# Two prices more in a kernel's scheduling model: VectorE's change of first partition and TensorE's change of weight width

## The chip, the cores and the metric

The kernel runs on one core of one Trainium2 chip. The metric is the device time of one execution in microseconds (us): 2971.12 as the median of three runs (2970.89 to 2973.47).

## What is computed

One layer of a decoder: a sequence of 2048 tokens of width 1024, a memory of 256 tokens. All is float32.

```
DEPTH = 1                                   # so layer 0 alone, the gated DeltaNet mixer
proj = x @ w_in                             # q, k, v, z (1024 each), a, b (8 each), mq (512)
qkv  = silu(causal_depthwise_conv(qkv, conv_w))
q, k = l2_normalize(q), l2_normalize(k)     # 8 heads of 128
o    = chunk_gated_delta_rule(q, k, v, g, beta)
       # in a chunk: A = I + strict_lower(beta k k^T * decay);  u = A^-1 v_beta,  w = A^-1 (k_beta e^g)
       # over chunks: state = state * dc + k_decay^T (u - w state)
o    = rms_norm(o, gate_norm_w) * silu(z)
m    = memory_attention(mq, mem_k, mem_v)   # 4 heads
x    = layer_norm(ALPHA * x + concat(o, m) @ w_out)
x    = layer_norm(ALPHA * x + square(relu(x @ w_ff1)) @ w_ff2)
```

## The kernel before

The tokens go through in four blocks of 512 (block 0 to 3). A block has a part of heads and a feed-forward part. In the heads part the projections aq, ak, av, az of eight heads (24 matmuls of 128x512 each, since every float32 product is made of three in float32r, from a high and a low part of each factor) alternate with small work of earlier heads. `dense` (line 671) makes a head's q, k, v, z; `gdn_a` (line 817) makes k k^T (pkq), the decays (dl, at) and calls `invert`; `gdn_b` (line 868) runs the recurrence over four chunks (pc, po, state). The memory attention (amq, sps, pmT, pmo) of four heads and the output projection (ao) fill in. The feed-forward part (af) uses a product scheme with seven instead of eight products.

`invert` (line 730) is the chain on which the prediction turns. VectorE copies blocks of L (tile dl) from four groups of 32 partitions into Lq, solves 16x16 blocks in fifteen steps of three operations (Bc, Bc, Xc), makes Z and its transpose ZT. Then three pairs of small matmul groups follow: pq = L-part times ZT, ScalarE copies pq to Q, pp = inverse-part times Q, and VectorE takes pp into ZT, Z, X, Y. The first pair has weights 112 columns wide, the second and third 64; all other matmul groups of the heads have 128. pp of the first pair needs Q and also XB, four copies of Z that ScalarE makes for four groups of 32 partitions. ScalarE makes much else in the same queue: the convolution's raw and scaled copies (raw, cq, ck, cv), squares with an accumulator (jq, jk), exponentials (dl, at, qd).

No engine's order is written by hand. Every operation is recorded (`Recorder.add`, line 147) with its engine, its tiles and a cost in ns; `Recorder.issue` (line 220) then plays the program through a model: it takes the engine that is free first, gives it the ready operation with the lowest number of recording, and notes start and end. An operation is ready when those that it depends on have ended plus a latency by pair of engines (`LAT`, `LAT_FROM`) and `MARGIN`. Tiles have so many buffers, and an operation waits for a free one. At the end all operations are sorted by modelled start (line 315) and emitted in this order (line 320), so that the model's times fix the order of each queue and nothing else. That is why every row of the profile has line 320. Semaphores make the real waits.

TensorE's cost is that of its columns plus, at a weight load, the time until the weights are in (lines 290 to 292). VectorE's is a constant and a price per element (line 211).

Of the kernel before, what the change touches and what calls it, by code (L numbers as in the profile page):

```python
# [14 lines left out]
P = 128  # L15
# [17 lines left out]
LAT = {("PE", "PE"): 0, ("DVE", "DVE"): 130, ("ACT", "ACT"): 155, ("POOL", "POOL"): 100}  # L33
LAT_FROM = {"PE": 200, "DVE": 130, "ACT": 135, "POOL": 75, "SP": 60}
MARGIN = 30


def _prod(v):
    r = 1
    for a in v:  # L40
        r *= a
    return r


class Buf:


    def __init__(self, pool, shape, dtype, tag, bufs, name):
        self.pool, self.shape, self.dtype, self.tag, self.bufs, self.name = pool, shape, dtype, tag, bufs, name
        self.ap = None  # L50
        self.psum = pool.name == "ps"
        self.users = 0
        self.end = 0
        self.held = False
        self.first = None
        self.log = []
# [7 lines left out]
class Ref:  # L64


    def __init__(self, buf, shape, steps=(), keys=None):
        self.buf, self.shape, self.steps, self.keys = buf, tuple(shape), steps, keys

    def _with(self, shape, *step):  # L70
        return Ref(self.buf, shape, self.steps + (step,), self.keys)

    def __getitem__(self, idx):
        ix = idx if isinstance(idx, tuple) else (idx,)
# [43 lines left out]
        return self._with(self.shape, "bitcast", (dt,), {})  # L118

    def part(self, *keys):  # L120
        return Ref(self.buf, self.shape, self.steps, frozenset(keys))

    def get(self):
        a = self.buf.get()
# [4 lines left out]

class Op:  # L130
    __slots__ = ("i", "eng", "fn", "args", "kw", "dur", "extra", "succ", "npred", "ready", "start", "end", "load", "last",
                 "bufs", "prio")


class Recorder:
# [11 lines left out]
    def add(self, eng, fn, name, args, kw):  # L147
        o = Op()
        o.i, o.eng, o.fn, o.args, o.kw = len(self.ops), eng, fn, args, kw
        o.succ, o.npred, o.ready, o.extra = [], 0, 0, 0  # L150
        o.prio = o.i + self.shift
        wr = [v for k, v in kw.items() if k in ("out", "accum_out")]
        rd = [v for k, v in kw.items() if k not in ("out", "accum_out")]
        rest = list(args)
        if "out" not in kw and rest:
            wr.append(rest.pop(0))
        rd += rest
        wr = [v for v in wr if isinstance(v, Ref)]
        rd = [v for v in rd if isinstance(v, Ref)]
        o.dur = self.cost(o, name, wr, rd, args, kw)  # L160
        preds = {}
        for refs, is_w in ((rd, False), (wr, True)):
            for r in refs:
                for q, qw, qk in r.buf.log:
                    if (is_w or qw) and (qk is None or r.keys is None or qk & r.keys):
                        preds[q.i] = q
        for refs, is_w in ((rd, False), (wr, True)):
            for r in refs:
                log = r.buf.log
                if is_w:  # L170
                    log[:] = [e for e in log if not (e[2] == r.keys or r.keys is None)]
                log.append((o, is_w, r.keys))
        for q in preds.values():
            q.succ.append(o)
        o.npred = len(preds)
        o.bufs = list({id(r.buf): r.buf for r in rd + wr}.values())
        for b in o.bufs:
            if b.first is None:
                b.first = o.i
            b.users += 1  # L180
        self.ops.append(o)

    @staticmethod
    def cost(o, name, wr, rd, args, kw):
        e = o.eng
        shapes = [r.shape for r in wr] + [r.shape for r in rd]
        n = max([_prod(s[1:]) for s in shapes] or [1])
        if e == "PE":
            rhs = kw.get("rhs", args[2])
            mo, n = _prod(args[1].shape[1:]), _prod(rhs.shape[1:])  # L190
            f32 = name == "transpose" or isinstance(rhs, Ref) and rhs.buf.dtype == F32
            o.load = 4 + 0.84 * mo
            o.last = 2.4 + 0.8334 * n if f32 else 13.4 + 0.4167 * n
            if name == "transpose":
                return o.last
            if f32:
                return o.last + max(o.last, o.load)
            return o.last
        psum = any(r.buf.psum for r in rd + wr)
        if e == "SP":  # L200
            o.extra = 1700 + _prod(wr[0].shape if wr else rd[0].shape) * 4 / 300.0
            return 450
        scal = [v for v in args[2:] if isinstance(v, Ref)] if name.startswith("tensor_scalar") else []
        scal += [v for k, v in kw.items() if k in ("scalar", "scalar1", "scale", "bias") and not isinstance(v, (int, float))]
        if e == "ACT":
            n = _prod((wr[0]).shape[1:])
            return 52 + 0.833 * n + (0 if psum else 42) + 93 * len(scal) + ((305 if scal else 198) if "accum_out" in kw else 0)
        if e == "DVE":
            fast = not psum and name in ("tensor_copy", "tensor_scalar_mul", "tensor_scalar_add", "tensor_scalar_max",
                                         "memset")  # L210
            return 68 + (0.52 if fast else 1.042) * n + 62 * len(scal) + (7 * n if name == "reciprocal" else 0)
        if name == "memset":
            return 40 + 0.83 * n
        if kw.get("op") == ALU.pow:
            return 300 + 165 * n
        if name == "tensor_copy":
            return 119 + 3.34 * n
        return 150 + 2.1 * n if name == "tensor_tensor" else 176 + 3.34 * n

    def issue(self):  # L220
# [3 lines left out]
        free = {e: 0.0 for e in engs}  # L224
        soon = {e: [] for e in engs}
        avail = {e: [] for e in engs}
        dma = [0.0]
        slots = {k: [0.0] * v[0].bufs for k, v in self.tags.items()}
        order = {k: sorted((b for b in v if b.users), key=lambda b: b.first) for k, v in self.tags.items()}
        pos = {}  # L230
# [18 lines left out]
        def place(o):  # L249
            for b in o.bufs:  # L250
                if not b.held:
                    if len(slots[b.key]) <= ahead(b):
                        wait[b.key].append(o)
                        return
                    b.held = True
                    b.since = heapq.heappop(slots[b.key])
                    again(b.key)
                o.ready = max(o.ready, b.since)
            heapq.heappush(soon[o.eng], (o.ready, o.i, o))

        def again(k):
            if wait[k]:
                w, wait[k] = sorted(set(wait[k]), key=lambda q: q.i), []
                for q in w:
                    pending.append(q)
# [4 lines left out]
        while True:  # L270
            while pending:
                place(pending.pop(0))
            best = None
            for e in engs:
                if avail[e]:
                    t = free[e]
                elif soon[e]:
                    t = max(free[e], soon[e][0][0])
                else:
                    continue  # L280
                if best is None or t < best[0]:
                    best = (t, e)
            if best is None:
                break
            t, e = best
            while soon[e] and soon[e][0][0] <= t:
                r, i, o = heapq.heappop(soon[e])
                heapq.heappush(avail[e], (o.prio, i, o))
            o = heapq.heappop(avail[e])[2]
            if e == "PE":  # L290
                t = max(t, fed + o.load)
                fed = t + o.dur - o.last
            o.start, o.end = t, t + o.dur
            free[e] = o.end
            if o.extra:
                dma[0] = max(o.end + 1700, dma[0]) + o.extra - 1700
                o.end = dma[0]
            out.append(o)
            for s in o.succ:
                lat = LAT.get((e, s.eng), LAT_FROM[e])  # L300
                if lat:
                    lat += MARGIN + (s.load if s.eng == "PE" else 0)
                s.ready = max(s.ready, o.end + lat)
                s.npred -= 1
                if s.npred == 0:
                    pending.append(s)
            for b in o.bufs:
                b.users -= 1
                b.end = max(b.end, o.end)
                if b.users == 0:  # L310
                    heapq.heappush(slots[b.key], b.end + LAT_FROM[e] + MARGIN)
                    again(b.key)
# [24 lines left out]
def hybrid_layer(  # L337
# [632 lines left out]
    def keep_sums(u, j):  # L970
# [9 lines left out]
        for i, o, x, y in ((1, 0, 1, 0), (3, 1, 3, 1), (2, 3, 3, 0), (4, 2, 2, 3)):  # L980
# [7 lines left out]
             ("S4", "B22", "A", True, (0, 1)))  # L988

    def ff_seven(b, ff1_tiles, relu2, add, norm2):  # L990
        Q = 2 * P
        for g in range(NS):
# [276 lines left out]
```

## Time and profile before

| | |
|---|---|
| median of 3 runs | 2971.12 us |
| the profiled execution | 2967.86 us |
| its span, first to last instruction | 2966.1 us |
| TensorE matmul busy | 2922.6 us, 99% |
| TensorE weight loads busy | 2410.1 us, 81% |
| VectorE busy | 2178.7 us, 73% |
| ScalarE busy | 1518.2 us, 51% |
| GpSimd busy | 342.1 us, 12% |
| chain that ended last: TensorE / VectorE / ScalarE | 81% / 8% / 7% |

A busy TensorE is not one at its peak: ends of matmuls are modelled, and they overlap. Where it matters, starts are compared. A wait is put down to the engine whose semaphore came last.

### The profile page before, as it was taken

To read this page: it belongs to the slowest core of one execution; us is meant where nothing else is said; L and a number is where in the kernel's file an instruction comes from. 1 tells how busy PE (TensorE), PEld (TensorE's weight loads), DVE (VectorE), ACT (ScalarE), POOL (GpSimd) and SP (SyncE) were. 2 spreads that over 40 slices of the span, in tenths; PEclk is the share of its full clock that TensorE was granted. 3 is DMA by queue.
4 is the path that set the end of the run, shared out by engine and by line. 5 is a ranking of instruction groups with operands and counts; after the bars stand their busy time and mean duration, and the time that the engine had idled before them with its cause. 6 is when DMAs were issued, how large, how long until landed. Compare 5 with 4: busy or idle time off the path is not lost.

```text
span 2966.1 us, 43768 instructions
## 1 busy us (share of the span) xinstructions
PE 2922.6 (99%) x15172; PEld 2410.1 (81%) x15172; DVE 2178.7 (73%) x5568; ACT 1518.2 (51%) x3582; POOL 342.1 (12%) x872
## 2 busy tenths in 40 slices
PE   8999999999999999999999999999999999999998
PEld 6888778888788878888888878888878887888886
DVE  7899887666888876665588777755668877675667
ACT  6666535444456652554545555344454556444443
POOL 2222100000122201000022220000001221000000
PEclk9999999999999999999999999999999999999999
DMA  8655577555733322544473333244456333324444
GB/s 283 238 192 178 192 237 234 194 190 181 278 136 121 121 100 79 158 146 137 154 258 135 122 111 100 89 144 148 149 168 244 125 122 111 100 86 149 145 146 135
DMA packets 127709, 469.84 MB, mean 158 GB/s; under 512 B 14464, under 2 KB 16896, under 8 KB 109056
## 3 DMA queue, kind: packets, MB, share of 16 engines
q1 hardware_dynamic: 126912, 467.00, 47.1%
q8 instruction: 119, 1.95, 0.3%
q14 instruction: 102, 0.84, 0.1%
q10 hardware_dynamic: 576, 0.06, 0.0%
HBM read 402.97 MB, written 64.03 MB: 157 GB/s over the span
## 4 chain that ended last, share of the span: by engine, by line
PE 81%; DVE 8%; ACT 7%; DMA 2%; issue 2%; POOL 1%; ACTq 0%; POOLq 0%; DVEq 0%
PE af L320 40%; PE ao L320 6%; PE az L320 5%; PE av L320 5%; PE ak L320 4%; PE aq L320 4%; PE amq L320 3%; PE pc L320 3%; DVE y L320 2%; PE pp L320 2%; PE pq L320 2%; PE po L320 2%; PE pkq L320 1%; DVE whl L320 1%; PE sps L320 1%
## 5 line engine op out<-in xcount | busy, mean ns | idle before, releaser
L320 DVE TENSOR_TENSOR whl<-wraw,whl 128x1024 fp32r<-128x1024 f32 (+1 forms) x446 | 541.4, 1216 | 462.6 <-ACT whl L320 460.9
L320 ACT CAST whl<-wraw 128x1024 fp32r<-128x1024 f32 (+1 forms) x446 | 466.6, 1046 | 371.7 <-PE af L320 202.6
L320 PE MATMUL af<-Thi,whl 128*128 128x512 f32 (+1 forms) x2304 | 649.8, 366 | 4.6 <-DVE whl L320 2.7
L320 PEld LDWEIGHTS af<-Thi,whl 128*128 128x128 f32 x2304 | 416.8, 189 | 76.0 <-DVE whl L320 3.7
L320 PE MATMUL af<-whl,xh 128*128 128x512 f32 x1536 | 474.8, 390 | 1.3 <-DVE whl L320 0.7
L320 PE MATMUL af<-Tlo,whl 128*128 128x512 f32 (+1 forms) x1152 | 421.1, 366 | 0.0
L320 PE MATMUL af<-whl,xl 128*128 128x512 f32 x896 | 346.0, 389 | 0.0
L320 PEld LDWEIGHTS af<-whl,xh 128*128 128x128 f32 x1536 | 287.8, 188 | 67.4 <-ACT whl L320 3.7
L320 PEld LDWEIGHTS af<-Tlo,whl 128*128 128x128 f32 x1152 | 217.3, 189 | 35.1
L320 PE MATMUL ao<-whl,ch 128*128 128x512 f32 x768 | 245.2, 397 | 0.3 <-DVE y L320 0.3
L320 ACT ACTIVATE rl<-af 128x512 f32<-128x512 f32 x128 | 76.5, 598 | 277.1 <-PE af L320 275.2
L320 PEld LDWEIGHTS af<-whl,xl 128*128 128x128 f32 x896 | 168.2, 188 | 34.4
L320 PE MATMUL aq<-Thi,whl 128*128 128x512 f32 x512 | 181.7, 412 | 7.2 <-ACT Thi L320 7.2
L320 PE MATMUL az<-Thi,whl 128*128 128x512 f32 x512 | 177.3, 406 | 1.1 <-DVE whl L320 1.1
L320 PE MATMUL av<-Thi,whl 128*128 128x512 f32 x512 | 176.6, 406 | 0.0
L320 PE MATMUL ak<-Thi,whl 128*128 128x512 f32 x512 | 173.5, 403 | 0.0
L320 PEld LDWEIGHTS ao<-whl,ch 128*128 128x128 f32 x768 | 143.1, 188 | 27.9 <-issue 1.4
L320 PE MATMUL ao<-whl,cl 128*128 128x512 f32 x384 | 156.2, 407 | 0.0
L320 DVE SCALAR_TENSOR_TENSOR y<-y,af 128x512 f32<-128x512 f32 x224 | 146.2, 677 | 8.7 <-PE af L320 8.7
L320 POOL MEMSET Y<- 128x512 f32 x32 | 16.8, 525 | 1037.9 <-PE af L320 921.0
L320 PEld LDWEIGHTS aq<-Thi,whl 128*128 128x128 f32 x512 | 94.7, 190 | 22.3 <-ACT Thi L320 7.2
L320 PEld LDWEIGHTS az<-Thi,whl 128*128 128x128 f32 x512 | 93.9, 189 | 17.3 <-DVE whl L320 1.5
(251 smaller groups left out, 5747.2 us busy)
## 6 DMA issues: line engine op xcount, KB each, us to landing
wraw<-in_w_ff_dram SPq DMA_DIRECT2D x224, 512.0 KB, 4.0
whl<-wsc SPq DMA_DIRECT2D x108, 1024.0 KB, 4.8
wraw<-tsc SPq DMA_DIRECT2D x128, 512.0 KB, 3.4
wsc<-whl SPq DMA_DIRECT2D x36, 1024.0 KB, 4.8
wraw<-in_w_out_dram SPq DMA_DIRECT2D x48, 512.0 KB, 4.2
wraw<-in_w_in_dram SPq DMA_DIRECT2D x35, 512.0 KB, 5.8
wq<-in_w_ff_dram SPq DMA_DIRECT2D x64, 256.0 KB, 4.4
tsc<-wq SPq DMA_DIRECT2D x64, 256.0 KB, 3.8
```

What stands on the lines that cost most here:

```text
L320: o.fn(*[res(a) for a in o.args], **{k: res(v) for k, v in o.kw.items()})
```

## The change

Two constants are added, DRAIN = 90 and SWITCH = 95 ns. A reference to a tile (`Ref`) now keeps the first partition of its slice (p0). An operation notes for its reads and writes, PSUM and SBUF apart, in which group of 32 partitions they begin (`quads`), and a matmul how many columns its weights have (`cols`). In `issue`, TensorE's start is put off by 95 ns when the width differs from that of the matmul before, and a VectorE operation whose group differs from the last one on the same side starts 90 ns after the engine is free. ScalarE, GpSimd and the queues are modelled as before.

```diff
+DRAIN, SWITCH = 90, 95
...
     def _with(self, shape, *step):
-        return Ref(self.buf, shape, self.steps + (step,), self.keys)
+        p0 = self.p0
+        if step[0] == "__getitem__":
+            ix = step[1][0]
+            ix = ix[0] if isinstance(ix, tuple) else ix
+            p0 += ix.indices(self.shape[0])[0] if isinstance(ix, slice) else 0
+        return Ref(self.buf, shape, self.steps + (step,), self.keys, p0)
...
+        o.quads = {("r" if v in rd else "w", v.buf.psum): v.p0 // 32 for v in wr + rd[::-1]}
...
-            o.load = 4 + 0.84 * mo
+            o.load, o.cols = 4 + 0.84 * mo, mo
...
+        quads, cols = {}, P
...
             if e == "PE":
+                if o.cols != cols:
+                    t += SWITCH
+                    cols = o.cols
                 t = max(t, fed + o.load)
                 fed = t + o.dur - o.last
+            if e == "DVE":
+                if any(quads.get(k, q) != q for k, q in o.quads.items()):
+                    t = max(t, free[e] + DRAIN)
+                quads.update(o.quads)
```

The instructions are the same in kind and number; their order differs in the heads of every block. Three places of block 3 follow, each as it was and as it is.

TensorE, first head of block 3, from its av projection to the first pair of the inversion (pq, then pp, 112 wide), before:

```order
L320 MATMUL av<-Tlo,whl 128x512
L320 MATMUL pq<-ZT_22859,LB 112x16 x4
L320 MATMUL av<-Thi,whl 128x512
L320 MATMUL az<-Thi,whl 128x512
L320 MATMUL az<-Tlo,whl 128x512
L320 MATMUL pp<-Q,XB 112x16 x4
L320 MATMUL az<-Thi,whl 128x512 x2
```

and now:

```order
L336 MATMUL av<-Tlo,whl 128x512
L336 MATMUL av<-Thi,whl 128x512
L336 MATMUL pq<-ZT_22859,LB 112x16 x4
L336 MATMUL az<-Thi,whl 128x512
L336 MATMUL az<-Tlo,whl 128x512
L336 MATMUL az<-Thi,whl 128x512 x2
L336 MATMUL az<-Tlo,whl 128x512
L336 MATMUL pp<-Q,XB 112x16 x4
```

The last av stands ahead of pq now, and five az instead of one av and two az stand between pq and pp.

ScalarE, at the same place (XB and Q are what pp waits for; raw and cv belong to the av projection), before:

```order
L320 COPY XB<-Z_22842 32x4x32 x2
L320 ACTIVATE th<-ck 128x512
L320 COPY XB<-Z_22842 32x4x32 x2
L320 COPY Q<-pq 112x4x16
L320 CAST kq<-ck 128x512
L320 COPY raw<-av 128x512
L320 ACTIVATE cv<-av,cw 128x512
```

and now:

```order
L336 COPY XB<-Z_22842 32x4x32 x2
L336 ACTIVATE th<-ck 128x512
L336 COPY XB<-Z_22842 32x4x32
L336 COPY raw<-av 128x512
L336 COPY XB<-Z_22842 32x4x32
L336 ACTIVATE cv<-av,cw 128x512
L336 COPY Q<-pq 112x4x16
L336 CAST kq<-ck 128x512
```

raw and cv have moved ahead of Q.

ScalarE, fourth head of block 3, the same copies (joss and jq are squares with an accumulator, on is the scaled output of an earlier head), before:

```order
L320 ACTIVATE joss,oss<-po 128x128
L320 ACTIVATE dl<-dl,gc 128x128
L320 COPY XB<-Z_23983 32x4x32
L320 ACTIVATE dl<-dl,gc 128x128
L320 COPY XB<-Z_23983 32x4x32
L320 ACTIVATE jq,ss<-ptq 128x128
L320 COPY XB<-Z_23983 32x4x32
L320 ACTIVATE jq,ss<-ptq 128x128
L320 COPY XB<-Z_23983 32x4x32
L320 ACTIVATE on<-po,ro 128x128
L320 COPY Q<-pq 112x4x16
```

and now:

```order
L336 ACTIVATE joss,oss<-po 128x128
L336 COPY XB<-Z_23977 32x4x32
L336 ACTIVATE dl<-dl,gc 128x128
L336 COPY XB<-Z_23977 32x4x32
L336 ACTIVATE dl<-dl,gc 128x128
L336 COPY XB<-Z_23977 32x4x32
L336 COPY Q<-pq 112x4x16
L336 ACTIVATE at<-at,ngc 128x128
L336 COPY XB<-Z_23977 32x4x32
L336 ACTIVATE jq,ss<-ptq 128x128
L336 ACTIVATE on<-po,ro 128x128
```

The two jq and on stand behind Q now, and one dl stands among the copies instead of ahead of them.

## Rows read from the trace of the kernel before

**Rows 1.** The page, busy us, share of the span and instructions by engine:

```profile
PE 2922.6 (99%) x15172; PEld 2410.1 (81%) x15172; DVE 2178.7 (73%) x5568; ACT 1518.2 (51%) x3582; POOL 342.1 (12%) x872
```

**Rows 2.** Windows (us), busy of PE, PEld, DVE, ACT, POOL, clock, DMA, GB/s:

```profile
480.00:720.00 240.00, 240.00 (x1060) 198.82 (x1059) 161.38 (x226) 116.34 (x157) 0.00 (x0) 1.00 0.61 198
...
2280.00:2520.00 240.00, 236.91 (x1428) 194.30 (x1427) 191.04 (x764) 140.40 (x490) 53.74 (x141) 1.00 0.34 122
```

**Rows 3.** Waits of TensorE, 2250 to 2590 us: us, times, longest:

```profile
PE pp L320 <- ACT Q L320: 1.4, 3, 0.6
PE pq L320 <- DVE Xc L320: 0.4, 1, 0.4
```

**Rows 4.** Waits of TensorE, 790 to 1130 us:

```profile
PE pq L320 <- DVE Bc L320: 0.4, 1, 0.4
```

**Rows 5.** Waits of TensorE, 60 to 400 us:

```profile
PE pp L320 <- ACT Q L320: 1.3, 3, 0.5
```

**Rows 6.** Waits of the weight loads, whole kernel:

```profile
PEld pp L320 <- ACT Q L320: 9.5, 15, 1.0
...
PEld pq L320 <- DVE Z L320: 3.2, 9, 0.7
```

**Rows 7.** Timeline of TensorE, a group 64 wide: start, us, operation, idle before:

```profile
2303.38 0.39 PE L320 MATMUL az<-Thi,whl 128*128 128x512 f32 x1
2303.70 0.65 PE L320 MATMUL pp<-Q,X 128*64 128x32 f32 x8
2304.28 0.50 PE L320 MATMUL az<-Thi,whl 128*128 128x512 f32 x1
2304.62 0.39 PE L320 MATMUL az<-Tlo,whl 128*128 128x512 f32 x1
```

**Rows 8.** Timeline of TensorE, first head of block 3, groups 112 wide:

```profile
2298.14 0.93 PE L320 MATMUL pq<-ZT,LB 128*112 128x16 f32 x8 [0.39 <-DVE Xc L320]
...
2299.47 0.40 PE L320 MATMUL az<-Tlo,whl 128*128 128x512 f32 x1
2299.70 0.87 PE L320 MATMUL pp<-Q,XB 128*112 128x16 f32 x8
2300.42 0.71 PE L320 MATMUL az<-Thi,whl 128*128 128x512 f32 x2
2300.97 0.40 PE L320 MATMUL az<-Tlo,whl 128*128 128x512 f32 x1
```

**Rows 9.** Timeline of VectorE, copies from groups of 32 partitions:

```profile
2291.15 0.27 DVE L320 COPY Lq<-dl 32x128 f32<-32x128 f32 x1
2291.29 0.20 DVE L320 TENSOR_TENSOR Xc<-Xc,Bc 128x52 f32<-128x52 f32 x1
2291.52 0.27 DVE L320 COPY Lq<-dl 32x128 f32<-32x128 f32 x1
```

**Rows 10.** Timeline of ScalarE, first head of block 3:

```profile
2299.11 0.21 ACT L320 COPY Q<-pq 112x64 f32<-112x64 f32 x1
...
2299.87 0.58 ACT L320 COPY raw<-av 128x512 f32<-128x512 f32 x1
2300.34 0.69 ACT L320 ACTIVATE cv<-av,cw 128x512 f32<-128x512 f32 x1
```

**Rows 11.** Timeline of ScalarE, fourth head of block 3:

```profile
2387.96 0.40 ACT L320 ACTIVATE dl<-dl,gc 128x128 f32<-128x128 f32 x1
2388.37 0.30 ACT L320 COPY XB<-Z 32x128 f32<-32x128 f32 x1
...
2389.21 0.29 ACT L320 COPY XB<-Z 32x128 f32<-32x128 f32 x1
...
2390.36 0.37 ACT L320 ACTIVATE on<-po,ro 128x128 f32<-128x128 f32 x1
```

**Rows 12.** Timeline of TensorE, fourth head of block 3:

```profile
2389.76 0.61 PE L320 MATMUL aq<-Thi,whl 128*128 128x512 f32 x2
2390.89 0.86 PE L320 MATMUL pp<-Q,XB 128*112 128x16 f32 x7 [0.52 <-ACT Q L320]
```

More of the change, by code (lines that the diff above doesn't have):

```diff
@@ L64, with __init__ @@
 class Ref:
-    def __init__(self, buf, shape, steps=(), keys=None):
-        self.buf, self.shape, self.steps, self.keys = buf, tuple(shape), steps, keys
+    def __init__(self, buf, shape, steps=(), keys=None, p0=0):
+        self.buf, self.shape, self.steps, self.keys, self.p0 = buf, tuple(shape), steps, keys, p0
     def _with(self, shape, *step):
-        return Ref(self.buf, shape, self.steps + (step,), self.keys)
+        p0 = self.p0
[4 more added lines that the diff above has]
+        return Ref(self.buf, shape, self.steps + (step,), self.keys, p0)
     def __getitem__(self, idx):
@@ L120, in part @@
     def part(self, *keys):
-        return Ref(self.buf, self.shape, self.steps, frozenset(keys))
+        return Ref(self.buf, self.shape, self.steps, frozenset(keys), self.p0)
     def get(self):
@@ L131 @@
     __slots__ = ("i", "eng", "fn", "args", "kw", "dur", "extra", "succ", "npred", "ready", "start", "end", "load", "last",
-                 "bufs", "prio")
+                 "bufs", "prio", "quads", "cols")
 class Recorder:
```

## The prediction

> **What bounds the kernel now.** I read the busy shares first, then windows by stage, then who waits for whom, then timelines of the places where a wait ends. TensorE is busy for 99% of the span, VectorE 73%, ScalarE 51% [rows 1]. The windows show two kinds of stage: in a feed-forward window TensorE is busy for 240.00 of 240 us and starts 1060 matmuls, one per 0.226 us; in a window of the heads it is busy 236.91 of 240 us [rows 2]. The granted clock is 1.00 in both, the 2.4 GHz level. So a better order can win something only in the heads, where TensorE waits for small chains: the inversion of a 128x128 block alternates matmul groups (pq, pp) with copies by ScalarE (Q, XB, Y) and with VectorE. From the order of the changed kernel this can be sharpened: on TensorE the feed-forward parts of blocks 1 to 3 stand row for row as before. What moves is the work of the heads.
>
> Who waits there: in the heads of block 3 the pp matmuls wait for ScalarE's Q three times, 1.4 us in all and 0.6 at most, and pq once for VectorE, 0.4 us [rows 3]; block 2 has the order of block 3. Block 1 does not wait for Q at all and 0.4 us at pq [rows 4], block 0 waits 1.3 us for Q [rows 5]. These are idle times left after modelled matmul ends. Weight loads, whose idle time starts earlier, show 9.5 us for Q and 3.2 us for VectorE's Z over the whole kernel [rows 6]. The truth lies between: at 2298.14 the page writes 0.39 us of idle, and at 2390.89 0.52 us [rows 8, 12]; the latter pp starts 1.13 us after a row of two matmuls began at 2389.76, and two matmuls take 0.45, so 0.68 was lost. A wait thus costs about 1.3 times its idle row.
>
> **The change part by part.** No instruction is added or removed; two prices are added to the model whose start times fix each engine's order.
>
> VectorE, 90 ns when the first partition changes. Normally a VectorE instruction starts before the one ahead of it ends: Xc at 2291.29 starts 0.13 us before the Lq copy of 2291.15 ends. The next Lq copy, from other partitions, starts at 2291.52, 0.03 us after Xc ended at 2291.49 [rows 9]. The change of partition costs 0.16 us against that neighbour, so the 90 ns are real and rather low. Some ten such changes per head (four Lq copies, two each of X32 and Y, one or two of X64 and of what follows) make about 1 us that the model left out and now has. [...]
>
> TensorE, 95 ns when the width of the weights changes. Around a group 64 wide, from the matmul at 2303.38 to the second one behind it at 2304.62, pass 1.24 us; two wide matmuls are 0.45 of it, the group from its start to its successor's 0.58, so 0.21 us goes for switching in and out against a charge of 0.19 [rows 7]. Around a group 112 wide, from 2299.47 to 2300.97, three wide matmuls are 0.68, the group 0.72, so 0.10 us is left against the same 0.19 [rows 8]. The 64-wide price is right, the 112-wide one about 0.09 us too high, twice a head. The Trainium skill, "TensorEngine Tiling (Array Packing)", section "Key Properties", says that a change of the tiling mode drains TensorE. A width of 112 needs no mode other than 128, so by this rule the charge there is unearned; the row, at half of the 64-wide cost, leans that way. The time that this would give is the slower rival below.
>
> What follows for the order, site by site in block 3 (block 2 has the same order):
>
> First head, TensorE and ScalarE. One av matmul moves ahead of pq, and five az matmuls instead of one av and two az stand between pq and pp. The wait of pq (0.39 us idle) loses up to 0.23. But ScalarE now puts raw and cv ahead of Q. Their runs are 0.58 and 0.69 us [rows 10]; some 1.1 to 1.3 us later than 2299.11 Q starts at 2300.2 to 2300.4 and ends 0.21 later. From Q's end at 2299.32 to pp at 2299.70 nothing was idle, so pp was not waiting; with two more matmuls in front it is due at 2300.15. It will wait 0.3 to 0.5 us. Net: a loss of 0.1 to 0.3, I take 0.2.
>
> Fourth head, ScalarE. Ahead of Q two jq with their accumulator reads, one on and one XB go; one dl comes in between. From 2388.37 to 2389.21 an XB with a jq takes 0.84, an XB alone runs 0.30, so a jq with its read takes 0.54; dl takes 0.41 to its successor, on runs 0.37 [rows 11]. The last XB, which pp needs as well, follows Q now. Up to its end 2 x 0.54 + 0.37 goes, one dl of 0.41 and one at of its kind come: 0.6 us earlier. TensorE has the same 1.1 us of work between pq and pp. The 0.52 us of idle [rows 12] goes; what is late next is pq two groups on, which has the X copies of VectorE ahead of it. Gain 0.5.
>
> Sixth head: ScalarE's order is as before, but one amq matmul more stands ahead of pq and one more between pq and pp, 0.45 us of cover against a wait of 0.4 to 0.6. Gain 0.4. Second head: order and wait stay, 0. In sum -0.7 us idle for a block, -1.4 for blocks 2 and 3.
>
> Block 1 had an order of its own without these waits and now gets that of blocks 2 and 3: it takes on the second head's 0.5, +0.5. Block 0: three waits, 1.3 us; the new order has more TensorE work ahead of pp at two of them. I take half, -0.7. Together -1.6 us of idle, times 1.3 is -2.1. The other small waits of the heads (pkq, pc, ptq) are shuffled with no reason that I can see for either sign; a chain that starts with more cover in most heads speaks for a little gain, and I take -3 in all. Bounds: if every wait of pq and pp went as the weight loads show them, 9.5 + 3.2, -12.7; if all that the 112-wide groups are overcharged became waiting, 0.09 x 2 x 32 = +5.8, and three first heads' 0.5 on top, +7.
>
> The profiled execution took 2967.86 us, 1.76 more than its span; the median of the runs is 2971.12, 3.3 above it. -3 gives 2964.9 in the first and 2968 in the second, and 2968 is the forecast.
>
> **The rivals.** Larger gain: with VectorE's prices right, most waits of the heads go, those of pkq and pc too, since they hang on the same late chain. For it: about 1 us per head was missing in the model and pq waits for VectorE only. Against it: the larger part of the wait is ScalarE's (9.5 against 3.2), and ScalarE is not charged for partition changes, though its jq with its accumulator read shows 0.54 us. Time: -7 to -13, centre 2961.
>
> Nothing: the model's two omissions, 1 us of VectorE and four 64-wide groups at 0.21, that is 0.84 us of TensorE per head, had nearly cancelled, and the new order is just another one. 2970 to 2973.
>
> Slower: ahead of the inversion's first two groups the model now thinks TensorE 0.09 us later per 112-wide group than it is, so that TensorE reaches pp early while Q is late; with raw and cv ahead of Q, as in the first head, in other heads too. It decides where pp has no slack of 0.2 us. Price +5.8 with the gains gone, up to +10: centre 2978.
>
> **How the numbers follow.** Forecast case 0.36, larger gain 0.31, nothing 0.13, slower 0.20. A measurement can tell 0.2%, 5.9 us, from no change. The larger gain lies wholly beyond that, the forecast case with 0.06 of its 0.36: faster 0.37. Slower 0.20 lies beyond on the other side. Within: 0.30 + 0.13 = 0.43. The range of the forecast alone is 2964 to 2971; with the two outer cases, until no more than 2 in 10 is out, 2956 to 2979.
>
> **What would show it.** Right: the fourth and sixth head of blocks 2 and 3 lose their idle before pp, the first head's pq waits less and its pp newly waits 0.3 to 0.5 us, block 1 looks like 2 and 3, and the feed-forward windows keep 0.226 us per matmul. Wrong: waits for Q as long as before or longer in the heads (then ScalarE's missing price or the 112-wide charge rules), or waits of pkq and pc that move by more than 2 us in total (then my shuffle term was not small).

## The result, and the profile after

The changed kernel took 2982.42 us (median of 5 runs, 2974.86 to 2987.02) against 2970.89 us for the kernel before in the same comparison: a ratio of 1.0037, 95% interval 1.0023 to 1.0052. It is slower by 0.4%, where 2968 us and a small gain were forecast. A second comparison gave 2979.08 us (8 runs; ratio 1.0026, 1.0014 to 1.0038); the median of all 13 is 2981.0. The profiled execution was the slowest of the first five, 2987.02 us, span 2985.3.

The page's busy line, which answers to [rows 1]:

```profile
PE 2933.9 (98%) x15172; PEld 2417.6 (81%) x15172; DVE 2179.3 (73%) x5568; ACT 1521.9 (51%) x3582; POOL 348.3 (12%) x872
```

The windows of [rows 2], with the same columns:

```profile
480.00:720.00 240.00, 240.00 (x1060) 198.70 (x1059) 162.38 (x228) 117.86 (x161) 0.00 (x0) 1.00 0.62 198
2280.00:2520.00 240.00, 236.51 (x1377) 194.67 (x1375) 195.53 (x773) 140.02 (x474) 52.07 (x139) 0.99 0.36 127
```

The feed-forward window is as it was, 1060 matmuls in 240 us. The window of the heads holds 1377 matmuls instead of 1428, and its granted clock is 0.99; the heads of block 3 begin 14 us later now, so the two windows do not hold the same stretch of them.

Waits of TensorE in the heads of block 3 (2265 to 2607 us), which answer to [rows 3]:

```profile
PE pp L336 <- ACT Q L336: 1.4, 3, 0.7
PE pkq L336 <- ACT jq L336: 0.9, 1, 0.9
PE ptq L336 <- ACT kd L336: 0.5, 1, 0.5
PE pp L336 <- ACT XB L336: 0.3, 1, 0.3
PE pq L336 <- DVE Bc L336: 0.2, 1, 0.2
```

Q is waited for exactly as long as before, 1.4 us in three places, which is the first of the signs by which the prediction said it would be wrong. pkq waited 0.4 us before and waits 0.9; ptq and a pp that waits for XB have come in addition. Blocks 1 and 2 have nearly the same rows.

The place of [rows 8, 10], the first head of block 3, ScalarE and then TensorE:

```profile
2314.34 0.29 ACT L336 COPY XB<-Z 32x128 f32<-32x128 f32 x1
2314.64 0.59 ACT L336 COPY raw<-av 128x512 f32<-128x512 f32 x1
2315.24 0.29 ACT L336 COPY XB<-Z 32x128 f32<-32x128 f32 x1
2315.55 0.69 ACT L336 ACTIVATE cv<-av,cw 128x512 f32<-128x512 f32 x1
2316.14 0.20 ACT L336 COPY Q<-pq 112x64 f32<-112x64 f32 x1
```

```profile
2314.02 0.93 PE L336 MATMUL pq<-ZT,LB 128*112 128x16 f32 x8 [0.22 <-DVE Bc L336]
...
2315.81 0.39 PE L336 MATMUL az<-Tlo,whl 128*128 128x512 f32 x1
2316.39 0.37 PE L336 MATMUL pp<-Q,XB 128*112 128x16 f32 x2 [0.19 <-ACT Q L336]
```

This is what was foretold: raw and cv stand ahead of Q, pq waits 0.22 instead of 0.39 us, and pp newly waits.

The second head of block 3, ScalarE and TensorE, where nothing was foretold:

```profile
2334.59 0.28 ACT L336 ACTIVATE jq<-ptq 128x128 f32<-128x128 f32 x1
2334.88 0.20 ACT L336 ACTIVATION_READ_ACCUMULATOR jq<-ptq 128x1 f32 x1
```

```profile
2333.75 0.47 PE L336 MATMUL aq<-Thi,whl 128*128 128x512 f32 x1
2335.14 0.38 PE L336 MATMUL pkq<-kq 128*128 128x256 f32 x1 [0.91 <-ACT jq L336]
```

pkq takes the PSUM bank that ptq had, so that the last jq must have read it. One aq matmul stands between pq and pkq; from its start to pkq pass 1.39 us, 1.16 more than it takes. That stands in blocks 1 to 3, 3.5 us together.

Where the time went can be read from starts: from the last af of one feed-forward part to the first af of the next is one part of heads. Block 1, before and in the second profile of the changed kernel (changed_again below):

```profile
777.44 0.39 PE L320 MATMUL af<-whl,xl 128*128 128x512 f32 x1
...
1164.18 0.28 PE L320 MATMUL af<-Thi,whl 128*128 128x256 f32 x1
```

```profile
781.97 0.39 PE L336 MATMUL af<-whl,xl 128*128 128x512 f32 x1
...
1174.31 0.28 PE L336 MATMUL af<-Thi,whl 128*128 128x256 f32 x1
```

That is 386.7 us before and 392.3 now. The heads of blocks 0 to 3 took 438.0, 386.7, 390.8 and 389.3 us before; 442.4, 392.3, 392.2 and 390.7 in this profile of the changed kernel, and 441.8, 395.5, 393.7 and 394.1 in the first. The feed-forward parts differ by 1.0 us at most. With half of every stretch at the lower clock taken out, block 1 lost 3.7 to 3.9 us and blocks 2 and 3 lost 1.2 to 1.4 each. Block 0 lost some 4, a part of it clock; its largest new waits (ao waited 0.3 us before and pto not at all) are these:

```profile
PE ao L336 <- DVE y L336: 2.3, 3, 1.5
PE pto L336 <- ACT on L336: 2.1, 2, 1.9
```

I use two measures below. The lost time of a group is its start minus the start of the matmul ahead, less what that one takes undisturbed (0.226 us for 128x512). The clock share of a run is its time times one minus its granted clock, which is what the lower level (1.2 GHz, shown as 0.5) takes from a TensorE that is always busy; a mean over the runs is given, since the clock is listed to 0.001. In every profile 5 to 9 us of it lie at the kernel's start and end, so only differences of it are read.

### The profile page after: what moved, and what is told of

It reads as the page before. It is cut to its first block, busy times and chain, and to the rows that moved or that the text cites. A ratio compares the mean times of both kernels' runs of the same rounds, so it can differ in the third digit from the quotient of the medians.

```text
span 2985.3 us, 43767 instructions
## 1 busy us (share of the span) xinstructions
PE 2933.9 (98%) x15172; PEld 2417.6 (81%) x15172; DVE 2179.3 (73%) x5568; ACT 1521.9 (51%) x3582; POOL 348.3 (12%) x872
## 4 chain that ended last, share of the span: by engine, by line
PE 79%; DVE 9%; ACT 6%; DMA 2%; POOL 2%; issue 2%; ACTq 0%; SPq 0%; POOLq 0%; DVEq 0%
PE af L336 40%; PE ao L336 6%; PE ak L336 5%; PE av L336 5%; PE az L336 4%; PE aq L336 4%; PE pc L336 2%; DVE y L336 2%; PE pp L336 2%; PE amq L336 2%; PE pq L336 2%; PE po L336 2%; PE pkq L336 1%; DVE whl L336 1%; ACT jq L336 1%
```

## The experiments

Three theories. A: ScalarE, whose partition changes stay free in the model, is where the chain is late, and waits close together pull the clock down. B: the charge at the 112-wide groups is too high, the model thinks TensorE later than it is, and gives it too little work ahead of pp (the prediction's slower rival). C: any other order would have cost as much.

| kernel | VectorE, ScalarE | 112, 64 wide | us (runs) | ratio, 95% | clock share | first pp lost |
|---|---|---|---|---|---|---|
| before | 0, 0 | 0, 0 | 2971 to 2972 (17 to 28 a comparison) | 1 | 11 | 7.2 |
| changed | 90, 0 | 95, 95 | 2981.0 (13) | 1.0037 and 1.0026 | 13 | 7.2 to 7.4 |
| drain_only | 90, 0 | 0, 0 | 2967.8 (12) | 0.9987 (0.9976 to 0.9999) | 13 | 5.8 |
| switch_only | 0, 0 | 95, 95 | 2988.2 (6) | 1.0049 (1.0032 to 1.0066) | 21 | 7.4 |
| drain_64 | 90, 0 | 0, 95 | 2971.6 (12) | 0.9998 (0.9988 to 1.0008) | 12 | 7.7 |
| drain_112 | 90, 0 | 95, 0 | 2980.3 (12) | 1.0029 (1.0018 to 1.0039) | 22 | 9.3 |
| dose_190 | 90, 0 | 190, 0 | 2990.8 (5) | 1.0065 (1.0052 to 1.0078) | 34 | 10.8 |
| as_rows | 90, 0 | 15, 135 | 2970.2 (11) | 0.9995 (0.9987 to 1.0004) | 11 | 5.4 |
| scalar_too | 90, 90 | 95, 95 | 2959.0 (6) | 0.9952 (0.9940 to 0.9964) | 7 | 2.5 |
| scalar_64 | 90, 90 | 0, 95 | 2955.2 (6) | 0.9939 (0.9926 to 0.9953) | 6 | 1.7 |
| scalar_vector | 90, 90 | 0, 0 | 2952.8 (6) | 0.9934 (0.9920 to 0.9947) | 8 | 1.0 |
| scalar_190 | 90, 90 | 190, 0 | 2968.5 (12) | 0.9993 (0.9982 to 1.0003) | 12 | 4.1 |

Prices are ns a change, "first pp lost" is us over the 32 heads, "before" without a column's price is the kernel itself.

**Which price.** drain_only and switch_only set one of the two to nothing.

```diff
-DRAIN, SWITCH = 90, 95
+DRAIN, SWITCH = 90, 0      # drain_only
+DRAIN, SWITCH = 0, 95      # switch_only
```

> Only VectorE's price (90 ns) is kept, TensorE's is 0. Theory A (the loss comes through ScalarE: VectorE's price makes the model think the chain of the inversion later, ScalarE fills the gap with raw and cv ahead of Q, and the waits that follow stand close together and pull TensorE's granted clock down): in the first heads raw, in block 1 also cv, still stands ahead of Q, so most of the loss stays, 2975 to 2983 us, with a granted clock of 0.994 to 0.996. Theory B (the overcharge of the 112-wide groups makes TensorE come to pp too early): without TensorE's price the loss goes, 2964 to 2971 us. Theory C (any other order costs about as much, the order of before was a lucky one): 2973 to 2980 us here and with TensorE's price alone too.

> Only TensorE's price (95 ns) is kept, VectorE's is 0. In the first heads of blocks 1 to 3 Q now stands right behind the XB copies on ScalarE. Theory A: no loss, 2966 to 2973 us, granted clock 0.997 to 0.998 as in the kernel before. Theory B: all of the loss, 2979 to 2985 us, with waits of pp for Q in most heads. Theory C: 2973 to 2980 us.

VectorE's price alone is a small gain, TensorE's alone all of the loss and more, 3 us above B's range: B is right in the sign of both. A had put the loss on the wrong price, though in drain_only raw still stands ahead of Q in the first heads.

drain_64 and drain_112 split TensorE's price by width, and dose_190 doubles it at the 112-wide groups:

```diff
-                if o.cols != cols:
+                mode = 64 if o.cols <= 64 else P       # drain_64
+                wide = 112 if o.cols == 112 else P     # drain_112
+                    t += 190 if 112 in (o.cols, cols) else 0    # dose_190
```

> Both prices, but TensorE's only where the width goes between up to 64 and above (the 112-wide groups are free). With VectorE's price alone the time was 2967.8 us, with both 2982.4. Theory B1 (of TensorE's price it is the 112-wide groups that do the harm: they show 0.10 us or less for 0.19 charged, and stand in the first pair of the inversion, where pp then comes too early): the loss goes, 2962 to 2970 us. Theory B2 (any charge on TensorE alone does harm as long as ScalarE's partition changes are free, since it is ScalarE that is late): the loss is still there, 2976 to 2985 us, with pp waiting for Q in the fourth and sixth heads for 0.7 us and more, and with raw and cv ahead of Q in the first head as its order shows.

> Both prices, but TensorE's only at the 112-wide groups; the 64-wide ones are free. Theory B1: the loss is here, 2976 to 2986 us. Theory B2: between, by the share of 140 of the 440 changes, 2968 to 2976 us.

> VectorE's price, and TensorE's at the 112-wide groups alone, doubled to 190 ns a change. VectorE's price alone took 2967.8 us, with 95 ns at these groups 2980.3. Theory B1 (the overcharge makes the model think TensorE later at pq and pp than it is, so that it puts too little work ahead of them): 0.19 us more for each of the groups, the lost time of pp behind Q grows from 9.3 us to 11 us or more, 2983 to 2993 us. Rival (the loss at 95 ns was one unlucky order): 2966 to 2980 us, and pp's lost time no longer than 9.3 us.

At the 112-wide groups 0, 95 and 190 ns give 2967.8, 2980.3 and 2990.8 us: the more is charged there, the more is lost. There are 64 such groups with a change in and out: 12.5 us over 64 is 0.195 us a group for 0.19 charged, 23.0 over 64 is 0.36 for 0.38. That these sizes agree does not show that the charge comes back as waiting: by the clock share 9 of the 12.5 us and 21 of the 23 are clock, and the first pp lost 3.5 and 5.0 us more. drain_64 ends 1.6 us above B's range, far below the rival's, and dose_190's first pp lost 10.8 us where 11 were expected. The waits of TensorE for Q over the whole kernel (us, times, longest), in the kernel before, the changed kernel, drain_only, drain_112 and dose_190, in this order:

```profile
PE pp L320 <- ACT Q L320: 4.2, 9, 0.6
```

```profile
PE pp L336 <- ACT Q L336: 4.9, 11, 0.7
```

```profile
PE pp L336 <- ACT Q L336: 2.7, 8, 0.5
```

```profile
PE pp L337 <- ACT Q L337: 6.4, 13, 0.7
```

```profile
PE pp L336 <- ACT Q L336: 7.2, 13, 0.8
```

The 64-wide price costs 3.8 us on top of VectorE's (2967.8 to 2971.6), which the two intervals do not tell from nothing, where a true price should have gained. One place is seen in the rows: in drain_64, as in the changed kernel, ptq lost 0.70 to 0.78 us in the first heads of blocks 1 to 3, and nothing there in drain_only and drain_112.

> VectorE's price, and TensorE's as the rows before have it, counted again: 15 ns a change at the 112-wide groups (0.03 us in and out beyond what the model has), 135 ns at the 64-wide ones (0.27 us). Theory B1 (only the part above the true cost does harm): 2963 to 2970 us, with pp's lost time at most that of VectorE's price alone, 5.8 us. Theory B2 (any more charge on TensorE does harm while ScalarE's own gaps are free): 2972 to 2980 us.

```diff
-                    t += SWITCH
+                    t += 15 if 112 in (o.cols, cols) else 135
```

With the charge at the 112-wide groups near what the rows show, the loss is gone: 2970.2 us, somewhat above B's upper end of 2970.

```diff
-MARGIN = 30
+MARGIN = 31        # margin_31; 90 in margin_90 below
```

> The kernel before with MARGIN 31 instead of 30 ns: no price, only another order (some 1100 of TensorE's printed rows differ from the kernel before, against 1800 in the changed kernel). It measures what a change of order is worth that follows no reason. Theory A and B: within 3 us of the kernel before, 2969 to 2975 us. Theory C (any other order loses, the one of before was lucky): 2975 to 2985 us.

margin_31 took 2969.1 us (11 runs; ratio 0.9996, 0.9987 to 1.0006): an order changed without a reason is not slower. C falls in its strong form, that any other order loses; one order is not every order, but drain_only and as_rows, two more, are not slower either.

**Is it cover?** Every dose also moves the other engines. Two kernels keep the modelled order and move rows of TensorE only, in the finished list (the edits are told in words here).

```diff
+# cover: changed kernel, first, fourth and sixth heads of blocks 1 to 3
+wide = the next two 128x512 matmuls behind pp
+out = out[:at of pp] + wide + the rest
+# uncover: drain_only, every head that has one
+wide = the last 128x512 matmul between pq and pp, put just behind pp
```

> The changed kernel; in the first, fourth and sixth heads of blocks 1 to 3, and there on TensorE alone, the next two 128x512 matmuls from behind the first pp go ahead of it (0.45 us of work). Every other row, and every other engine, stays as in the changed kernel. In these nine places pp lost 0.38, 0.42 and 0.82 us by its starts. Theory B1 (what is lost is cover: TensorE has too little to do between pq and pp): 3 x (0.38 + 0.42 + 0.45) = 3.7 us less, 2974 to 2979 us against 2979 to 2982 of the changed kernel. Rival (the chain is late anyway, a pp that starts later passes its wait on to the next pair): 2979 to 2984 us.

> The kernel with VectorE's price alone (2967.8 us), its order kept, but for one 128x512 matmul in every head, which goes from between the first pq and pp to just behind pp: 0.226 us less cover in each head, about what the 112-wide charge takes away by being too high (0.16 us a group). Theory B1: pp's lost time grows from 5.8 us by 0.1 to 0.2 in most heads, to 9 or 11 us, and the time to 2972 to 2981 us, part of it as a lower granted clock (0.9956 now). Rival (only the reshuffle behind the charge did harm, not the cover): 2966 to 2970 us.

uncover took 2981.2 us (8 runs; ratio 1.0032, 1.0021 to 1.0043) against 2967.8. 28 of the 32 heads have such a matmul, and in three of them the next one went along: 31 matmuls, 7.0 us less work ahead of pp, cost 13.4, about as much as the changed kernel lost against drain_only. By the clock share (16 against 13) 3 of it are clock. The lost time ahead of the first pp went from 5.8 to 10.1 us, and of the second pair's pq from 4.2 to 5.7. Its waits, against the 2.7 us of drain_only above:

```profile
PE pp L350 <- ACT Q L350: 5.8, 13, 0.7
...
PE pq L350 <- DVE ZT L350: 2.2, 8, 0.5
```

cover took 2978.8 us (11 runs; ratio 1.0022, 1.0012 to 1.0032), 2.2 below the changed kernel's 2981.0, where B wanted 3.7. That is just inside B's range, and not clear of the noise (the runs go from 2971.1 to 2983.9); the clock share is 10 against 13, so no waiting is seen to be gone in sum: the first pp's lost time fell from 7.2 to 3.5 us as foretold, but pq of the second pair rose from 3.6 or 4.0 to 6.8. The rival is right for most of it: a chain that ScalarE finishes late passes its wait on.

```profile
PE pp L345 <- ACT Q L345: 3.3, 8, 0.7
...
PE pq L345 <- DVE ZT L345: 2.2, 7, 0.4
```

So too little cover is enough to make a loss of this size, and cover given back at nine places alone does not undo it. That it makes the whole loss of the changed kernel is not shown: of the 13 us against drain_only the first pp lost only 1.5 more, at the same clock share, and the rest lies in many places, those of block 0 among them.

> The kernel before with MARGIN 90 instead of 30 ns and no price: every result counts as 60 ns later for whoever waits for it on another operation, so that more of TensorE's work is put between pq and pp. With 31 ns the time was 2969.1 us. If work ahead of pp is what counts, whatever gives it: 2955 to 2966 us, and pp's lost time below the 6.9 us of the kernel before. Rival (only right prices at the right operations help): 2967 to 2978 us.

margin_90 took 2966.0 us (12 runs; ratio 0.9981, 0.9972 to 0.9989), at the very end of what was expected, with 3.5 us lost ahead of the first pp. More cover without any price helps, less than ScalarE's price does, though MARGIN moves the other engines' order too; part of it goes at another place, af waiting for VectorE's weights, 3.4 us before:

```profile
PE af L320 <- DVE whl L320: 10.6, 5, 3.0
```

**ScalarE.** The XB and Y copies follow each other every 0.31 us in the trace of the kernel before (median of 82 such pairs), and the model has 0.20. scalar_too charges ScalarE as VectorE:

```diff
-            if e == "DVE":
+            if e in ("DVE", "ACT"):
```

> The changed kernel with a third price: ScalarE too is charged 90 ns when the first partition changes (its XB and Y copies follow each other every 0.31 us in the trace, where the model has 0.20). Theory A (what was missing was ScalarE's price, the other two prices alone make ScalarE look free): the waits for Q and of pkq behind jq get shorter, 2963 to 2971 us, granted clock 0.997 or more. Theory B: TensorE's overcharge is still there, 2978 to 2985 us. Theory C (just one more order): 2973 to 2982 us.

scalar_64, scalar_vector and scalar_190 have this edit and TensorE's price as in drain_64, drain_only and, at the 112-wide groups, dose_190; scalar_vector_60 has MARGIN 60.

> VectorE's and ScalarE's price for the partition, and TensorE's for the 64-wide groups alone. The kernel with all three prices took 2959.0 us. Theory B1 (the 112-wide charge is wrong wherever it stands): faster still, 2953 to 2958 us. Theory B2 (with ScalarE charged nothing is left to gain by it): 2957 to 2963 us.

> VectorE's and ScalarE's price, none for TensorE. Theory B1: TensorE's price at the 64-wide groups is right and missing here, 2960 to 2966 us. Theory B2: TensorE's price does harm by itself, 2950 to 2958 us.

> VectorE's and ScalarE's price, and 190 ns at the 112-wide groups alone. Without TensorE's price this took 2952.8 us; without ScalarE's price the 190 ns cost 23 us (2967.8 to 2990.8). If the overcharge does harm by itself: 2962 to 2976 us. If it does harm only where ScalarE is late with Q: 2952 to 2958 us.

> VectorE's and ScalarE's price, none for TensorE (2952.8 us), with MARGIN 60 instead of 30 ns. The first pp loses only 1.0 us in all there, so little is left to cover. If more margin still helps: 2945 to 2951 us; if the cover is enough already and a longer chain only makes the heads late: 2953 to 2962 us.

ScalarE's price gains 22 us on the changed kernel (2981.0 to 2959.0, 4 below A's range) and 15 on drain_only; scalar_vector, at 2952.8 us, beats both kernels. It has no wait of pp for Q left among its rows (the sixth head of block 3, TensorE, from the first pq to pp):

```profile
2446.78 0.87 PE L337 MATMUL pq<-ZT,LB 128*112 128x16 f32 x8
...
2449.87 0.38 PE L337 MATMUL pp<-Q,XB 128*112 128x16 f32 x3
```

Here TensorE has 3.09 us of work from pq to pp. The same head before, and in the changed kernel:

```profile
2460.49 0.87 PE L320 MATMUL pq<-ZT,LB 128*112 128x16 f32 x8
...
2462.74 0.96 PE L320 MATMUL pp<-Q,XB 128*112 128x16 f32 x8 [0.59 <-ACT Q L320]
```

```profile
2477.13 0.87 PE L336 MATMUL pq<-ZT,LB 128*112 128x16 f32 x8
...
2479.66 0.96 PE L336 MATMUL pp<-Q,XB 128*112 128x16 f32 x8 [0.66 <-ACT Q L336]
```

Against scalar_vector, TensorE's prices cost again: 2.4 us for the 64-wide (not clear of the noise), 6.2 for both, 15.7 for 190 ns at the 112-wide (scalar_64 came out in B1's range, scalar_vector in B2's: without the 112-wide price it is faster, without any faster still). So the overcharge does harm by itself, not only where ScalarE is late. scalar_vector_60 took 2952.7 us (6 runs; ratio 0.9935, 0.9921 to 0.9948): the first pp loses 0.6 us there, and more cover has nothing left to give, nor did it cost anything.

```diff
-DRAIN, SWITCH = 90, 95
+DRAIN, SWITCH = 110, 95     # and 15 or 135 for SWITCH, as in as_rows
-... + ((305 if scal else 198) if "accum_out" in kw else 0)
+... + (93 if "accum_out" in kw else 0)
```

> All prices as the rows of the trace have them: 110 ns for a change of partition on VectorE and ScalarE, 15 ns for TensorE's change at 112 wide and 135 ns at 64, 93 ns instead of 198 or 305 for ScalarE's accumulator read. If the model is the better the nearer its prices are: 2946 to 2953 us. If the too high accumulator was cushion for ScalarE's chain: 2954 to 2962 us.

all_rows took 2979.3 us (8 runs; ratio 1.0025, 1.0015 to 1.0034), a miss: it is the slowest of those that charge ScalarE. But not all of its prices were nearest the rows. From a read of the accumulator to kd pass 0.09 us, as priced; from the read of one jq to the next jq pass 0.22 to 0.23 (62 times in its trace, and 20 times with joss), so that ScalarE was priced some 0.13 too low there:

```profile
2291.52 0.20 ACT L337 ACTIVATION_READ_ACCUMULATOR jq<-ptq 128x1 f32 x1
2291.74 0.28 ACT L337 ACTIVATE jq<-ptq 128x128 f32<-128x128 f32 x1
```

Its top wait is new:

```profile
PE ptq L337 <- ACT kd L337: 7.4, 9, 2.3
```

ptq waits for kd, which stands behind the jk whose accumulator reads were made cheaper. That their old price was cushion is argued from this row; three prices were changed at once, and which of them did it is open.

**The clock.** Between the two profiled runs I first read the loss as clock: in the changed kernel three stretches at 0.5 (10.2 us at 850.6, 6.8 at 1584.5, 6.8 at 2482.2) against one of 3.4 us before. Two of them began 0.8 us behind the pp of a first head. q_first removes that wait alone: XB and Q go ahead of raw and cv.

```diff
+        for q, late in self.late:        # late: raw and cv of the av projection
+            ... put late, and what hangs on it, just behind q
```

> The changed kernel, with raw and cv moved behind Q on ScalarE in the first heads of blocks 1 to 3 and nothing else moved: TensorE, VectorE and the queues have the order of the changed kernel. By their starts the pp groups of these heads lost 0.38, 0.38 and 0.36 us. Theory A (these waits pull the granted clock down behind them, at 850.6 us for 10.2 us and at 1584.5 us for 6.8 us in the changed kernel): the waits go and with them the two stretches at the low clock, 1.1 + 8.5 = about 9 us less than the changed kernel, 2971 to 2976 us, granted clock 0.997. Rival (the low clock comes where it comes, whatever stands on ScalarE): only the waits themselves go, 1.1 us, 2979 to 2983 us, granted clock 0.995.

> The changed kernel once more, for a second profile. If the low clock belongs to the waits of its order, at least two of the three stretches come again at the same places (first head of block 1 and 2, sixth head of block 3: about 850, 1584 and 2482 us). If not, they stand elsewhere. Time 2977 to 2986 us.

q_first took 2979.3 us (12 runs; ratio 1.0021, 1.0012 to 1.0029), 1.6 below the changed kernel, which is within the noise: it fits the rival's 1.1 and not A's 9. And the second profile of the changed kernel has full clock where the first had not. Three windows, the first of the changed kernel's first profile, then two of its second:

```profile
840.00:870.00 30.00, 29.55 (x149) 22.93 (x147) 22.91 (x109) 12.96 (x40) 3.61 (x11) 0.83 0.32 117
```

```profile
840.00:870.00 30.00, 28.66 (x173) 22.89 (x171) 24.07 (x117) 15.82 (x52) 4.25 (x13) 1.00 0.32 118
...
1010.00:1025.00 15.00, 14.35 (x97) 11.70 (x96) 7.07 (x26) 9.29 (x35) 3.31 (x9) 0.89 0.25 96
```

The places do not come again; A falls here too. Over 13 runs the changed kernel's clock share is 13 us against 11: of its ten us, eight are not clock.

## Why the prediction was wrong

The step that failed first is the one on TensorE's price: "The 64-wide price is right, the 112-wide one about 0.09 us too high, twice a head", put aside as a rival at +5.8 us and up. The mechanism of that rival, a charge too high there that leaves too little work ahead of pp, is what the runs show, and its size was too small. The group of [rows 8] has eight passes that the model already counts, 8 x 0.098 = 0.78 us, so of 1.50 us only 0.04 is left beyond three wide matmuls, not 0.10: some 0.15 of the 0.19 was too much, and the rival's own sum gives 0.15 x 2 x 32 = 9.6 us instead of 5.8. Measured, 95 ns there cost 12.5 us (8 to 17 by the two intervals), 9 of them clock, which the rival did not have. By the same count the 64-wide price was not right but too low: eight passes of 0.058 us, as the trace has them, are 0.46 of the 1.24 us of [rows 7], which leaves 0.33 against 0.19. The Trainium skill, "TensorEngine Tiling (Array Packing)", section "Key Properties", names a change of tiling mode as what drains TensorE; the trace agrees, since the 112-wide group, which needs none, shows 0.04 us. It was the price there that did the harm.

The forecast case itself, -3 us, failed in every block. It had -0.7 us for block 0, +0.5 for block 1 and -0.7 for each of blocks 2 and 3; the starts show losses of some 4, of 3.7 to 3.9 and of 1.2 to 1.4 each.

The second step that failed is "the other small waits of the heads (pkq, pc, ptq) are shuffled with no reason that I can see for either sign". By their starts, the places at the kernel's start left out, ptq lost 0.6 us before and 2.5 after, about 0.75 in each of the three first heads where it had lost nothing. pkq lost 4.3 and 5.1, at new places (1.16 in each of three second heads), and pc lost less, 8.1 and 6.3. The mark I had set, 2 us for pkq and pc, is not reached by these sums. ptq and pkq wait for ScalarE (kd, jq), which I had named as uncharged and then used only against the larger gain. The wait of pkq is not what tells the changed kernel from the faster drain_only, which has it too in blocks 2 and 3, 1.04 us each. pto in block 0, 2.1 us, was not on my list at all.

The third is the sixth head: "one amq matmul more stands ahead of pq and one more between pq and pp, 0.45 us of cover", gain 0.4. The amq are there (2.53 instead of 2.25 us from pq to pp), and the wait stayed, 0.66. ScalarE sets it: from the first XB copy of the chain to Q it takes 2.56 us in both kernels (2459.91 to 2462.47, 2476.84 to 2479.40), and pq started 0.58 us behind that copy before and 0.29 behind it now. TensorE came earlier by as much as it had been given more to do. I had counted matmuls between two rows of TensorE, not where TensorE stands against the chain. In block 1 this weighed most: its order of before had lost 0 and 0.10 us at the fourth and sixth heads' first pp, and the new one loses 0.40 and 0.82.

What held: the feed-forward parts; block 1 takes the order of blocks 2 and 3; the first head's trade (by starts pq 0.55 to 0.39, pp 0 to 0.38 in blocks 2 and 3). The fourth head's first pp went from 0.68 to 0.43 us, half of what I took, because an exponential (at) stands ahead of the last XB copy and pp now waits for that; its second pp newly lost 0.6. The second head, taken as 0, gained 0.5, and pkq there took 1.16 back. VectorE's price held: alone it gained about 4 us (0.3 to 7 by the interval).

That leaves the clock, which the prediction took as 1.00 throughout. For this change it is 2 of 10 us; at dose_190 it is 21 of 23. Why the same lost cover turns into waits in one order and into clock in another stays open.

## What to carry to other kernels

In a planner, a price too high on the engine that bounds the kernel can be worse than one too low: it takes work away from between a result and its use. 95 ns where the rows show 0.02 a change cost 12.5 us; the 64-wide price left out, 0.33 us a group too low, cost nothing that the runs can tell. Look for the engine of a chain that has no price at all: the largest gain here, 22 us, lay in the engine that the change left out. And read a moved consumer against the chain that it waits for, not against the rows around it on its own engine.

## What the runs showed of the hardware

In 20 profiles TensorE's granted clock fell to 0.5 (the 1.2 GHz level) in 51 stretches of 3.4 to 13.7 us, the kernel's start and end left out, and each began behind or in waits of TensorE, of 0.5 to 3.2 us together; behind 29 of them this was one pp or pkq alone, with 0.60 to 1.4 us lost. Not every such wait does it: the sixth heads' pp, 0.8 us in each block, was followed by a low stretch in one of three blocks in the first profile of the changed kernel and in two in its second. ScalarE, too, takes longer where the first partition changes. In the trace of the kernel before, the first of a chain's four XB copies, which begins on partition 0, takes 0.19 us to a next instruction that begins there too; from one XB copy to the next, and from the other three to an instruction that begins on partition 0, mostly 0.31 to 0.32 pass.
